# A two-layer backbone on one core: the up-projections of both feed forwards by seven products of halves

## The chip, the core and the metric

The kernel runs on one core of a Trainium2 chip. The engines of the core have queues of their own and wait for each other by semaphores: PE (TensorE) multiplies, with its weight loads shown as PEld; DVE (VectorE), ACT (ScalarE) and POOL (GpSimd) work on tiles; DMAs are issued from SP's queue. The metric is the device time of one execution in microseconds, lower is better, as the median of several runs.

## The reference

Two layers over 512 latent and 256 context tokens of width 1024. Each layer normalizes, projects, mixes the tokens in three ways, merges, and then has a gated feed forward with a convolution of width 3 along the tokens:

```python
def conv_ffn(xn, w_up, conv_w, w_down):
    u = dwconv(xn @ w_up, conv_w)
    a, gt = jnp.split(u, 2, axis=-1)
    return (a * jax.nn.silu(gt)) @ w_down
...
        h_lat = h_lat + m_lat[5] * conv_ffn(modulate(rmsnorm(h_lat, norm2_w[l]), m_lat[3], m_lat[4]),
                                            w_up[l], ffn_conv_w[l], w_down[l])
        if need_ctx:
            h_ctx = h_ctx + m_ctx[5] * conv_ffn(...)
```

w_up is 1024 x 5632 (the half a and the half of the gates), w_down 2816 x 1024. All data are float32. In the first layer the feed forward takes all 768 tokens, in the last only the 512 latent ones.

## The kernel before

A float32 product is made of three matmuls. Every operand x is split into h, its rounding to the type fp32r (a cast on ACT), and l = x - h (a subtraction on DVE, or on POOL where the code says so); the matmuls are weights h with tokens h, weights h with tokens l, weights l with tokens h, summed in one PSUM bank. `split` and `wsplit` do this; `wraw` (L213) loads the raw weights by a DMA into one of three buffers, and the halves of the weights go to two buffers each (`wh`, `wl`).

The feed forward (`ffn`) works feature-major: a block is 128 columns of w_up for all tokens. 22 blocks of gates (g) and 22 of a are done in pairs, in groups of four blocks of the hidden width (`FG`); the names are f0 or f1 for the layer, g or a, and the number of the pair's first block, with the group first: f1a42 is layer 1, a, group 4, third and fourth block. The order is g00, a00, g02, a02, g40, d0, a40, g42, a42, g80, d4, a80 and so on to a200, d16 and the tail: after the first gate pair of a group comes the down product d of the group before, added to the residual (`done_d`, L1734). The first pair, g00, is done by `gemm_first`, which takes the features one by one as the norm gives them out (`norm_fin`: t on DVE L619, xh on ACT L621, xl on DVE L622); the other 21 pairs of a layer by `gemm_fm`: for each block raw weights, split, and in `mm3` (matmuls L248 to L250) eight blocks of the contraction, three matmuls each, for 512 latent columns and in layer 0 again for 256 context columns.

```python
            for k in range(nk):
                nc.tensor.matmul(o, hv[:, k, :], xh[:, k, :], start=(k == 0), stop=False)
                nc.tensor.matmul(o, hv[:, k, :], xl[:, k, :], start=False, stop=False)
                nc.tensor.matmul(o, lv[:, k, :], xh[:, k, :], start=False, stop=(k == nk - 1))
```

A block's result is taken from PSUM by `conv`: ACT writes the middle tap (L1699), DVE adds the two others (L1700, L1702). Gates go through silu on ACT (L1708); for a, POOL multiplies with the gate (L1714), and ACT and DVE split the product into gh and gl (L1715, L1716). A scheduler orders the instructions of each engine at build time by priorities; on the chip every engine runs its list in order and waits where an operand or a buffer isn't there. In the first four pairs of layer 0's feed forward a unit of the next modulation (adp, adc) lies between.

## Time and profile before

| what | value |
|---|---|
| runs | 2727.49, 2726.53, 2725.04 us, median 2726.53 |
| span of the profiled execution | 2715.6 us |
| median of the runs above that span | 10.9 us |
| busy in the span: PE, DVE, ACT, POOL | 98%, 58%, 37%, 9% |

The profiled execution is another one than the runs; its time is given by its span, from the first to the last instruction, and the runs count 10.9 us more that lie around a span. Differences that are worked out from the trace are taken to move the runs by as much. A busy share is a mean over all stages; the feed forwards, from about 1008 to 1568 us (layer 0) and from about 2332 us to the end (layer 1), have to be looked at by themselves.

### The profile page before, as it was taken

Reading aid. Unit: us, or ns where it says so; the run is one execution under the profiler, and the core shown is the slowest. Engines: PE = TensorE matmul, PEld = TensorE weight load, DVE = VectorE, ACT = ScalarE, POOL = GpSimd, SP = SyncE. Lnnn points to the kernel's source line nnn. Section 1 sums busy time; section 2 is a strip of 40 time slices with the busy share of each in tenths; the row PEclk is TensorE's granted clock in tenths of the full one; section 3 lists DMA queues with packets and bytes.
Section 4 is the critical chain, followed back from the end, with each engine's and each line's share of the span. In section 5 each row is a group of like instructions: output and inputs, shape, how many; then the busy total and the mean of one; then the engine's idle time right before and its main releaser. Section 6 shows DMA issues by size and latency. Waiting matters only on the chain.

```text
span 2715.6 us, 46016 instructions
## 1 busy us (share of the span) xinstructions
PE 2663.0 (98%) x18041; PEld 2261.6 (83%) x18041; DVE 1573.4 (58%) x3527; ACT 998.5 (37%) x2269; POOL 235.0 (9%) x234
## 2 busy tenths in 40 slices
...
DMA packets 523466, 342.97 MB, mean 126 GB/s; under 512 B 48007, under 2 KB 488561, under 8 KB 522481
## 3 DMA queue, kind: packets, MB, share of 16 engines
...
## 4 chain that ended last, share of the span: by engine, by line
PE 88%; DMA 5%; DVE 3%; ACT 1%; issue 1%; SPq 1%; POOL 0%; DVEq 0%; ACTq 0%; POOLq 0%
PE mg04p L249 2%; PE mg04p L250 2%; PE adp L467 2%; PE mg04p L248 2%; PE y0p L248 1%; PE y0p L250 1%; PE y0p L249 1%; PE mg14p L248 1%; PE mg14p L250 1%; PE mg14p L249 1%; PE y1p L248 1%; PE y0op L248 1%; PE y0op L250 1%; PE y0op L249 1%; PE y1p L249 1%
## 5 line engine op out<-in xcount | busy, mean ns | idle before, releaser
L1714 POOL TENSOR_TENSOR f0a<-f0a,f0g 128x768 f32<-128x768 f32 x22 | 40.7, 1848 | 486.8 <-DVE f0a L1702 486.8
L467 PE MATMUL adp<-ad,s 128*32 128x128 f32 x1280 | 65.5, 283 | 2.7 <-DVE cz0t L903 2.4
L1714 POOL TENSOR_TENSOR f1a<-f1a,f1g 128x512 f32<-128x512 f32 x22 | 28.5, 1294 | 315.4 <-DVE f1a L1702 284.4
L467 PEld LDWEIGHTS adp<-ad,s 128*32 128x32 f32 x1280 | 33.9, 110 | 26.0 <-issue 9.9
L1716 DVE TENSOR_TENSOR f0gl<-f0a,f0gh 128x768 fp32r<-128x768 f32 x22 | 21.1, 959 | 58.4 <-ACT f0gh L1715 58.4
L1715 ACT CAST f0gh<-f0a 128x768 fp32r<-128x768 f32 x22 | 18.3, 832 | 76.6 <-POOL f0a L1714 76.6
L1638 POOL TENSOR_TENSOR y0a<-y0a,y0g 128x768 f32<-128x768 f32 x16 | 33.0, 2062 | 129.9 <-DVE y0g L1635 127.6
L470 ACT COPY adr<-adp 128x128 f32<-128x128 f32 x80 | 21.2, 265 | 39.7 <-PE adp L467 39.3
L901 ACT ACTIVATE mg0t<-mg04p 128x512 f32<-128x512 f32 (+1 forms) x40 | 19.4, 486 | 38.5 <-PE mg04p L250 28.2
L1708 ACT ACTIVATE f0g<-f0g 128x768 f32<-128x768 f32 x22 | 18.5, 845 | 33.2 <-DVE f0g L1702 33.2
L1638 POOL TENSOR_TENSOR y1a<-y1a,y1g 128x512 f32<-128x512 f32 x16 | 23.9, 1494 | 78.3 <-DVE y1g L1635 78.3
L491 DVE TENSOR_REDUCE ada<-adc 128x2 f32<-128x8 f32 x80 | 12.9, 161 | 27.9 <-PE adc L489 27.6
L1635 DVE SCALAR_TENSOR_TENSOR y0g<-y0g,y0p 128x512 f32<-128x512 f32 (+1 forms) x32 | 17.4, 549 | 15.7 <-PE y0p L250 14.7
L1708 ACT ACTIVATE f1g<-f1g 128x512 f32<-128x512 f32 x22 | 13.8, 631 | 32.9 <-DVE f1g L1702 32.9
L979 DVE SCALAR_TENSOR_TENSOR m0mb<-m0mb,g0a,cst 128x128 f32<-128x128 f32 x48 | 14.0, 346 | 18.4 <-DMA m0mb<-g0rd 18.4
L489 PE MATMUL adc<-cst,adr 128*128 128x128 f32 x80 | 22.2, 278 | 0.4 <-ACT adr L470 0.4
L1659 DVE SCALAR_TENSOR_TENSOR hr<-y0op,y0gh,hr 128x512 f32<-128x512 f32 (+1 forms) x16 | 9.8, 615 | 21.0 <-PE y0op L250 21.0
L1002 PE MATMUL m0n<-m0vb,m0mb 128*128 128x129 f32 x96 | 19.1, 299 | 1.1 <-issue 1.1
L1611 DVE TENSOR_TENSOR y0l<-y0ld,y0h 128x768 fp32r<-128x768 f32 x12 | 13.0, 1093 | 12.2 <-ACT y0h L1610 12.2
L1734 DVE SCALAR_TENSOR_TENSOR hr<-f0d8p,ada,hr 128x512 f32<-128x512 f32 (+1 forms) x16 | 9.9, 618 | 15.7 <-PE f0d8p L250 15.7
L1734 DVE SCALAR_TENSOR_TENSOR hr<-f0d12p,ada,hr 128x512 f32<-128x512 f32 (+1 forms) x16 | 9.9, 618 | 15.7 <-PE f0d12p L250 15.7
L1734 DVE SCALAR_TENSOR_TENSOR hr<-f0d4p,ada,hr 128x512 f32<-128x512 f32 (+1 forms) x16 | 9.9, 618 | 15.7 <-PE f0d4p L250 15.7
...
## 6 DMA issues: line engine op xcount, KB each, us to landing
...
```

The lines of the kernel that those rows point to most:

```text
L248: nc.tensor.matmul(o, hv[:, k, :], xh[:, k, :], start=(k == 0), stop=False)
L249: nc.tensor.matmul(o, hv[:, k, :], xl[:, k, :], start=False, stop=False)
L250: nc.tensor.matmul(o, lv[:, k, :], xh[:, k, :], start=False, stop=(k == nk - 1))
L467: nc.tensor.matmul(ps[32 * j:32 * j + 32, 0:128], self.s32[:, 2 * k:2 * k + 32], raw[:, k, :], start=(k < 4), stop=(k >= 4), tile_position ...
L470: nc.scalar.copy(rw, ps[:, 0:128])
L489: nc.tensor.transpose(ps[:, 128:256], rw, self.ident)
L901: nc.scalar.activation(s, o, AF.Tanh, scale=0.5)
L1638: nc.gpsimd.tensor_tensor(out=a[:, :nt], in0=a[:, :nt], in1=gt[:, :nt], op=ALU.add)
L1708: nc.scalar.activation(a[:, :nt], a[:, :nt], AF.Silu)
L1714: nc.gpsimd.tensor_tensor(out=a[:, :nt], in0=a[:, :nt], in1=keep[b][:, :nt], op=ALU.mult)
L1716: nc.vector.tensor_tensor(out=gl[:, k, :nt], in0=a[:, :nt], in1=gh[:, k, :nt].bitcast(F32), op=ALU.subtract)
L1734: nc.vector.scalar_tensor_tensor(out=hv[:, a:b], in0=ps, scalar=self.ada[l][:, 40 + j, (a >= SEQ):(a >= SEQ) + 1], in1=hv[:, a:b], op0=ALU ...
```

## The change

A pair of blocks is one product of a matrix of 2 x 2 blocks: the contraction in two halves (k blocks 0 to 3 and 4 to 7), the columns in two (the blocks r0 and r1), and the tokens in two (t0, t1; 384 each in layer 0, 256 in layer 1). `gemm7` does it in seven products of halves, after Strassen, in place of eight, with twelve matmuls each. For this POOL makes sums of the weights' halves (`half`, L314: s23 twice, r1 in place, s4, of 128x512 each), which are split like other weights: w0 = r0, w23, w1 = r1 of 1024 columns, w4 of 512. The products go to the PSUM banks x1, x6, x7, x5, and five additions on DVE (L348, L350, L354, L356, L358) and two copies on ACT (L346, L352) make the two blocks c in SBUF from them, which `conv` (now L1795, L1796, L1798) reads. The sums of the tokens are made once per layer: `norm_fin` writes the unsplit features too (L721, on POOL), `norm_sums` makes the sums T of them (eight subtractions, L620) and splits them (four times 128 x 2nt on ACT and DVE). `wh` and `wl` get a third buffer; the slots of 3072 columns become twelve of 1536 (`q6`); `first_weights` puts its weights into `wh` and `wl`. Comments are removed, and `dynamic_dma_scratch_size=1024` is set.

```diff
+class Blocks:
+
+    def __init__(self, tiles, a, b):
+        self.tiles, self.a, self.b = tiles, a, b
+
+    def __getitem__(self, i):
+        _, k, t = i
+        a = self.a + (t.start or 0)
+        b = self.b if t.stop is None else self.a + t.stop
+        return self.tiles[k // 2][:, k % 2, a:b]
...
-    def y12(self, name, dt=F32):
-        return self.P([128, 3072], name, "y12", 4, dt)
-
-    def acc(self, name, dt=F32):
-        return self.P([128, 3072], name, "acc", 2, dt)
+
+    def q6(self, name, dt=F32):
+        return self.P([128, 1536], name, "q6", 12, dt)
+
+    def pairs(self, name, n, dt=F32):
+
+        return [self.q6(f"{name}{i}", dt).rearrange("p (k t) -> p k t", k=2) for i in range(n)]
...
-            h = self.T([128, 1024], f"{nm}h", F32R, tag="wh", bufs=2)
-            l = self.T([128, 1024], f"{nm}l", F32R, tag="wl", bufs=2)
+            h = self.T([128, 1024], f"{nm}h", F32R, tag="wh", bufs=3)
+            l = self.T([128, 1024], f"{nm}l", F32R, tag="wl", bufs=3)
...
+    def gemm7(self, src, c0, x, nt, done, nm):
+        nc = self.nc
+        n = nt // 2
+        xh, xl, th, tl = x
+        r0, r1 = [self.wraw(src[:, c0 + 128 * b:c0 + 128 * b + 128], KD, 128, f"{nm}r{b}") for b in range(2)]
+        s23 = self.P([128, KD, 128], f"{nm}s23", "s23", 1)
+        s4 = self.P([128, 4, 128], f"{nm}s4", "s4", 1)
+        lo, hi = slice(0, 4), slice(4, 8)
+        def half(out, a, b, op):
+            with self.high(self.prio):
+                nc.gpsimd.tensor_tensor(out=out, in0=a, in1=b, op=op)
+        half(s23[:, hi], r0[:, lo], r1[:, lo], ALU.subtract)
+        half(r1[:, lo], r1[:, lo], r1[:, hi], ALU.add)
+        half(s23[:, lo], r1[:, lo], r0[:, lo], ALU.subtract)
+        half(s4, r0[:, hi], s23[:, lo], ALU.subtract)
+        w0 = self.wsplit(r0, KD, 128, f"{nm}w0")
+        w23 = self.wsplit(s23, KD, 128, f"{nm}w23")
+        w1 = self.wsplit(r1, KD, 128, f"{nm}w1")
+        w4 = self.wsplit(s4, 4, 128, f"{nm}w4")
+        def prod(ps, w, o, h, l, start, stop):
+            mm = lambda a, b, **kw: nc.tensor.matmul(ps, a, b, skip_group_check=True, **kw)
+            for k in range(4):
+                mm(w[0][:, o + k, :], h(k), start=(start and k == 0), stop=False)
+                mm(w[0][:, o + k, :], l(k), start=False, stop=False)
+                mm(w[1][:, o + k, :], h(k), start=False, stop=(stop and k == 3))
+        def of(t, k0, c):
+            return [lambda k, v=v: v[:, k0 + k, c] for v in t]
+        def oft(p0, c):
+            return [lambda k, v=v: v[p0 + k // 2][:, k % 2, c] for v in (th, tl)]
+        t0, t1 = slice(0, n), slice(n, nt)
+        x1, x7 = self.pl(f"{nm}x1")[:, 0:n], self.pl(f"{nm}x7")[:, 0:n]
+        x6, x5 = self.pb(f"{nm}x6")[:, 0:n], self.pb(f"{nm}x5")[:, 0:n]
+        c = [self.st(f"{nm}c{b}") for b in range(2)]
+        u = self.st(f"{nm}u")
+        p1, u2, u3 = u[:, 0:n], u[:, n:2 * n], c[1][:, 0:n]
+        add = dict(op=ALU.add)
+        prod(x1, w0, 0, *of((xh, xl), 0, t0), True, True)
+        nc.scalar.copy(p1, x1)
+        prod(x6, w23, 0, *oft(2, t1), True, True)
+        nc.vector.tensor_tensor(out=u2, in0=x6, in1=p1, **add)
+        prod(x7, w23, 4, *oft(0, t1), True, True)
+        nc.vector.tensor_tensor(out=u3, in0=x7, in1=u2, **add)
+        prod(x1, w0, 4, *of((xh, xl), 4, t0), False, True)
+        nc.scalar.copy(c[0][:, t0], x1)
+        prod(x5, w1, 0, *oft(0, t0), True, True)
+        nc.vector.tensor_tensor(out=c[1][:, t1], in0=x5, in1=u3, **add)
+        prod(x7, w1, 4, *oft(2, t0), False, True)
+        nc.vector.tensor_tensor(out=c[1][:, t0], in0=x7, in1=u2, **add)
+        prod(x5, w4, 0, *of((xh, xl), 4, t1), False, True)
+        nc.vector.tensor_tensor(out=c[0][:, t1], in0=x5, in1=u2, **add)
+        for b in range(2):
+            done(b, [(c[b][:, a:e], (a, e)) for a, e in ((0, SEQ), (SEQ, nt)) if e > a])
+            self.ada_next()
...
+        xh, xl, xs = self.x48(nm, nt)
+        self.N = dict(nm=nm, l=l, which=which, acc=self.st(f"{nm}acc"), xs=xs, x=(xh, xl), nt=nt)
+        if which:
+            self.N["raw"] = self.pairs(f"{nm}R", 4)
...
+    def norm_sums(self):
+        nc, N = self.nc, self.N
+        nt, nm, R = N["nt"], N["nm"], N["raw"]
+        t0, t1 = slice(0, nt // 2), slice(nt // 2, nt)
+        def sub(out, a, b):
+            nc.vector.tensor_tensor(out=out, in0=a, in1=b, op=ALU.subtract)
+        th, tl = [None] * 4, [None] * 4
+        def split(i):
+            th[i], tl[i] = [self.pairs(f"{nm}T{v}{i}", 1, F32R)[0] for v in "hl"]
+            self.split(th[i][:, :, :nt], tl[i][:, :, :nt], R[i][:, :, :nt])
+        for p in range(2):
+            a, b = R[p], R[p + 2]
+            sub(a[:, :, t0], a[:, :, t1], a[:, :, t0])
+            sub(a[:, :, t1], b[:, :, t1], a[:, :, t1])
+            sub(b[:, :, t1], b[:, :, t1], a[:, :, t0])
+            sub(b[:, :, t0], b[:, :, t0], b[:, :, t1])
+        for i in (2, 3, 0, 1):
+            split(i)
+        return (*N["x"], th, tl)
...
+            if "raw" in N:
+                nc.gpsimd.tensor_scalar(out=N["raw"][j // 2][:, j % 2, a:b], in0=t, scalar1=B[:, j, s:s + 1],
+                                        scalar2=None, op0=ALU.add)
...
-            gh = self.y12(f"{nm}gh{f0}", F32R).rearrange("p (k t) -> p k t", k=4)
-            gl = self.y12(f"{nm}gl{f0}", F32R).rearrange("p (k t) -> p k t", k=4)
+            gh, gl = [], []
...
                 def done_a(b, ps):
                     a = conv(f0 + p0 + b, ps, f"a{f0}{p0}{b}")
-                    k = p0 + b
+                    if b == 0:
+                        gh.extend(self.pairs(f"{nm}gh{f0}{p0}", 1, F32R))
+                        gl.extend(self.pairs(f"{nm}gl{f0}{p0}", 1, F32R))
+                    h = gh[-1][:, b, :nt]
                     nc.gpsimd.tensor_tensor(out=a[:, :nt], in0=a[:, :nt], in1=keep[b][:, :nt], op=ALU.mult)
-                    nc.scalar.copy(gh[:, k, :nt], a[:, :nt])
-                    nc.vector.tensor_tensor(out=gl[:, k, :nt], in0=a[:, :nt], in1=gh[:, k, :nt].bitcast(F32),
-                                            op=ALU.subtract)
-
-                n = min(2, fn - p0)
+                    nc.scalar.copy(h, a[:, :nt])
+                    nc.vector.tensor_tensor(out=gl[-1][:, b, :nt], in0=a[:, :nt], in1=h.bitcast(F32), op=ALU.subtract)
+
                 if f0 + p0 == 0:
                     self.gemm_first(KD, xs, done_g, f"{nm}g{f0}{p0}")
+                    x7 = self.norm_sums()
                 else:
-                    self.gemm_fm(U, D_FF + 128 * (f0 + p0), 128 * n, KD, xs, done_g, f"{nm}g{f0}{p0}")
+                    self.gemm7(U, D_FF + 128 * (f0 + p0), x7, nt, done_g, f"{nm}g{f0}{p0}")
                 if down and f0 + FG < NFF:
                     self.gemm_fm(*down)
                     down = None
-                self.gemm_fm(U, 128 * (f0 + p0), 128 * n, KD, xs, done_a,
-                             f"{nm}a{f0}{p0}")
-            segs = [((a, b), gh[:, :, a:b], gl[:, :, a:b]) for a, b in segb]
+                self.gemm7(U, 128 * (f0 + p0), x7, nt, done_a, f"{nm}a{f0}{p0}")
+            segs = [((a, b), Blocks(gh, a, b), Blocks(gl, a, b)) for a, b in segb]
```

On DVE, layer 1, from the end of pair a40 on (before; L205 is a low half of weights, L1716 gl, L1700 and L1702 the conv, whose second operand f1..p is the PSUM bank):

```order
L205 TENSOR_TENSOR f1a42s0l<-f1a42r_24754,f1a42s0h 128x1024
L1700 SCALAR_TENSOR_TENSOR f1g_24713<-f1g42p_0_24688,vec,f1g_24713 128x511
L1716 TENSOR_TENSOR f1gl_24373<-f1a_24675,f1gh_24372 128x512
L1702 SCALAR_TENSOR_TENSOR f1g_24713<-f1g42p_0_24688,vec,f1g_24713 128x511
L205 TENSOR_TENSOR f1a42s1l<-f1a42r_24792,f1a42s1h 128x1024
L1700 SCALAR_TENSOR_TENSOR f1g_24749<-f1g42p_0_24724,vec,f1g_24749 128x511
L1702 SCALAR_TENSOR_TENSOR f1g_24749<-f1g42p_0_24724,vec,f1g_24749 128x511
L205 TENSOR_TENSOR f1g80s0l<-f1g80r_24832,f1g80s0h 128x1024
L1700 SCALAR_TENSOR_TENSOR f1a_24785<-f1a42p_0_24760,vec,f1a_24785 128x511
L1702 SCALAR_TENSOR_TENSOR f1a_24785<-f1a42p_0_24760,vec,f1a_24785 128x511
```

and in the changed kernel, in pair g42 (L218 are low halves of weights, L1815 is gl, L1796 and L1798 the conv, of c; x is a PSUM bank, u and c are in SBUF):

```order
L348 TENSOR_TENSOR f1g42u<-f1g42x_25400,f1g42u 128x256
L1798 SCALAR_TENSOR_TENSOR f1a_25356<-f1a40c_25262,vec,f1a_25356 128x511
L218 TENSOR_TENSOR f1g42w4l<-f1g42s_25377,f1g42w4h 128x512
L1798 SCALAR_TENSOR_TENSOR f1a_25365<-f1a40c_25263,vec,f1a_25365 128x511
L350 TENSOR_TENSOR f1g42c_25403<-f1g42x_25399,f1g42u 128x256
L354 TENSOR_TENSOR f1g42c_25403<-f1g42x_25401,f1g42c_25403 128x256
L218 TENSOR_TENSOR f1a42w0l<-f1a42r_25506,f1a42w0h 128x1024
L1815 TENSOR_TENSOR f1gl_25361<-f1a_25356,f1gh_25360 128x512
L356 TENSOR_TENSOR f1g42c_25403<-f1g42x_25399,f1g42u 128x256
L218 TENSOR_TENSOR f1a42w23l<-f1a42s_25510,f1a42w23h 128x1024
L1815 TENSOR_TENSOR f1gl_25361<-f1a_25365,f1gh_25360 128x512
L358 TENSOR_TENSOR f1g42c_25402<-f1g42x_25401,f1g42u 128x256
```

Additions from PSUM now stand between the low halves of the next weights, and the conv reads c.

On POOL, layer 1, the products with the gates were all that it had in the pairs:

```order
L1714 TENSOR_TENSOR f1a_24637<-f1a_24637,f1g_24405 128x512
L1714 TENSOR_TENSOR f1a_24675<-f1a_24675,f1g_24441 128x512
L1714 TENSOR_TENSOR f1a_24785<-f1a_24785,f1g_24713 128x512
L1714 TENSOR_TENSOR f1a_24823<-f1a_24823,f1g_24749 128x512
L1714 TENSOR_TENSOR f1a_25095<-f1a_25095,f1g_24863 128x512
```

and now from pair g42's halves on (r are the raw weights, s is s23 or s4):

```order
L314 TENSOR_TENSOR f1g42s_25376<-f1g42r_25372,f1g42r_25374 128x512
L314 TENSOR_TENSOR f1g42r_25374<-f1g42r_25374 128x512
L314 TENSOR_TENSOR f1g42s_25376<-f1g42r_25374,f1g42r_25372 128x512
L314 TENSOR_TENSOR f1g42s_25377<-f1g42r_25372,f1g42s_25376 128x512
L314 TENSOR_TENSOR f1a42s_25510<-f1a42r_25506,f1a42r_25508 128x512
L314 TENSOR_TENSOR f1a42r_25508<-f1a42r_25508 128x512
L314 TENSOR_TENSOR f1a42s_25510<-f1a42r_25508,f1a42r_25506 128x512
L1813 TENSOR_TENSOR f1a_25356<-f1a_25356,f1g_25062 128x512
L314 TENSOR_TENSOR f1a42s_25511<-f1a42r_25506,f1a42s_25510 128x512
L1813 TENSOR_TENSOR f1a_25365<-f1a_25365,f1g_25067 128x512
L314 TENSOR_TENSOR f1g80s_25650<-f1g80r_25646,f1g80r_25648 128x512
L314 TENSOR_TENSOR f1g80r_25648<-f1g80r_25648 128x512
```

The four halves of a pair stand ahead of or between the products of the pair before.

On DVE, layer 0, between the last step of the norm (L723, before L622) and the first addition of a00, the changed kernel has among others these (R are the unsplit features, T their sums):

```order
L620 TENSOR_TENSOR n01R_10625<-n01R_10625 128x2x384
...
L620 TENSOR_TENSOR n01R_10626<-n01R_10626,n01R_10624 128x2x384
L218 TENSOR_TENSOR f0a00w23l<-f0a00s_11317,f0a00w23h 128x1024
L620 TENSOR_TENSOR n01R_10626<-n01R_10626 128x2x384
L218 TENSOR_TENSOR f0a00w1l<-f0a00r_11315,f0a00w1h 128x1024
L218 TENSOR_TENSOR n01Tl_11298<-n01R_10625,n01Th_11297 128x1536
L218 TENSOR_TENSOR f0a00w4l<-f0a00s_11318,f0a00w4h 128x512
...
L218 TENSOR_TENSOR n01Tl_11302<-n01R_10626,n01Th_11301 128x1536
L218 TENSOR_TENSOR n01Tl_11306<-n01R_10623,n01Th_11305 128x1536
L218 TENSOR_TENSOR n01Tl_11310<-n01R_10624,n01Th_11309 128x1536
L348 TENSOR_TENSOR f0a00u<-f0a00x_11341,f0a00u 128x384
```

where before, behind the conv of g00, the conv of a00 began:

```order
L1700 SCALAR_TENSOR_TENSOR f0g_11248<-f0g00p_1_11095,vec,f0g_11248 128x255
L1702 SCALAR_TENSOR_TENSOR f0g_11240<-f0g00p_1_11094,vec,f0g_11240 128x255
L1702 SCALAR_TENSOR_TENSOR f0g_11248<-f0g00p_1_11095,vec,f0g_11248 128x255
L1700 SCALAR_TENSOR_TENSOR f0a_11312<-f0a00p_0_11262,vec,f0a_11312 128x511
L1702 SCALAR_TENSOR_TENSOR f0a_11312<-f0a00p_0_11262,vec,f0a_11312 128x511
L205 TENSOR_TENSOR f0g02s0l<-f0g02r_11417,f0g02s0h 128x1024
```

So x6 of a00, whose addition is the last row of the changed kernel, comes behind w23 and the first two T.

## Rows read from the trace of the kernel before

**Rows 1.** The page: span, and busy time by engine.

```profile
span 2715.6 us, 46016 instructions
PE 2663.0 (98%) x18041; PEld 2261.6 (83%) x18041; DVE 1573.4 (58%) x3527; ACT 998.5 (37%) x2269; POOL 235.0 (9%) x234
```

**Rows 2.** Windows of the two feed forwards, each row start:end, length, then the engines' busy time.

```profile
1060.00:1560.00 500.00, 500.00 (x3006) 433.31 (x3005) 233.80 (x350) 140.22 (x209) 36.97 (x20) 1.00 0.26 75
2360.00:2660.00 300.00, 300.00 (x1295) 242.72 (x1294) 154.01 (x197) 103.32 (x146) 25.89 (x20) 1.00 0.32 94
```

**Rows 3.** Timeline of PE at the starts of two pairs, layer 1: start, duration, engine, line.

```profile
2428.85 0.39 PE L248 MATMUL f1g42p<-n11xh,f1g42s0h 128*128 128x512 f32 x1
...
2440.05 0.39 PE L248 MATMUL f1a42p<-n11xh,f1a42s0h 128*128 128x512 f32 x1
```

**Rows 4.** Timeline of PE, context columns of a pair of layer 0.

```profile
1195.54 0.28 PE L248 MATMUL f0a42p<-n01xh,f0a42s1h 128*128 128x256 f32 x1
...
1196.50 0.28 PE L250 MATMUL f0a42p<-n01xh,f0a42s1l 128*128 128x256 f32 x1
```

**Rows 5.** Timeline of DVE in the pairs of layer 1.

```profile
2429.90 1.23 DVE L205 TENSOR_TENSOR f1g42s1l<-f1g42r,f1g42s1h 128x1024 fp32r<-128x1024 f32 x1 [2.93 <-ACT f1g42s1h L204]
2431.05 0.68 DVE L1716 TENSOR_TENSOR f1gl<-f1a,f1gh 128x512 fp32r<-128x512 f32 x1
2431.65 0.74 DVE L1700 SCALAR_TENSOR_TENSOR f1a<-f1a40p,vec,f1a 128x511 f32<-128x511 f32 x1
...
2458.13 0.74 DVE L1700 SCALAR_TENSOR_TENSOR f1g<-f1g80p,vec,f1g 128x511 f32<-128x511 f32 x1
2458.79 0.68 DVE L1716 TENSOR_TENSOR f1gl<-f1a,f1gh 128x512 fp32r<-128x512 f32 x1
```

**Rows 6.** Lines of POOL, shapes apart: line, operation, count, busy us, mean ns, idle before.

```profile
L1714 POOL TENSOR_TENSOR f0a<-f0a,f0g 128x768 f32<-128x768 f32 x22 | 40.7, 1848 | 486.8 <-DVE f0a L1702 486.8
L1714 POOL TENSOR_TENSOR f1a<-f1a,f1g 128x512 f32<-128x512 f32 x22 | 28.5, 1294 | 315.4 <-DVE f1a L1702 284.4 <-issue 31.0
L546 POOL TENSOR_TENSOR n01acc<-n01acc,n01sq 128x256 f32<-128x256 f32 x9 | 6.6, 736 | 15.2 <-ACT n01sq L545 9.8 <-DVE n01acc L546 5.4
```

**Rows 7.** The page, costliest groups: the low half of the gate's product, layer 0.

```profile
L1716 DVE TENSOR_TENSOR f0gl<-f0a,f0gh 128x768 fp32r<-128x768 f32 x22 | 21.1, 959 | 58.4 <-ACT f0gh L1715 58.4
```

**Rows 8.** Timelines of POOL and DVE at two places of the merge, layer 0.

```profile
878.68 1.85 POOL L1638 TENSOR_TENSOR y0a<-y0a,y0g 128x768 f32<-128x768 f32 x1 [2.32 <-DVE y0g L1635]
879.15 2.46 DVE L205 TENSOR_TENSOR y0s21l<-y0r,y0s21h 128x1024 fp32r<-128x1024 f32 x1 [0.55 <-ACT y0s21h L204]
...
905.52 1.22 DVE L205 TENSOR_TENSOR y0s10l<-y0r,y0s10h 128x1024 fp32r<-128x1024 f32 x1
905.68 2.76 POOL L1638 TENSOR_TENSOR y0a<-y0a,y0g 128x768 f32<-128x768 f32 x1 [1.74 <-DVE y0g L1635]
907.45 1.02 DVE L1635 SCALAR_TENSOR_TENSOR y0g<-y0g,y0p 128x512 f32<-128x512 f32 x2 [0.71 <-issue]
```

**Rows 9.** Timeline of DVE, norm and first pair: layer 0, then layer 1.

```profile
1007.23 0.87 DVE L619 SCALAR_TENSOR_TENSOR n_0t<-hr,modA,n_0rb 128x256 f32<-128x256 f32 x2
...
1029.70 0.87 DVE L622 SCALAR_TENSOR_TENSOR n01xl<-n_512t,ada,n01xh 128x256 fp32r<-128x256 f32 x2
...
1034.11 0.87 DVE L1700 SCALAR_TENSOR_TENSOR f0g<-f0g00p,vec,f0g 128x255 f32<-128x255 f32 x2 [1.56 <-ACT f0g L1699]
1034.90 0.86 DVE L1702 SCALAR_TENSOR_TENSOR f0g<-f0g00p,vec,f0g 128x255 f32<-128x255 f32 x2
...
2330.53 0.87 DVE L619 SCALAR_TENSOR_TENSOR n_0t<-hr,modA,n_0rb 128x256 f32<-128x256 f32 x2
...
2345.62 1.27 DVE L622 SCALAR_TENSOR_TENSOR n11xl<-n_256t,ada,n11xh 128x256 fp32r<-128x256 f32 x3
```

**Rows 10.** Timeline of PE: first product of the second gate pair, layer 0, layer 1.

```profile
1049.25 0.50 PE L248 MATMUL f0g02p<-n01xh,f0g02s0h 128*128 128x512 f32 x1
...
2362.07 0.40 PE L248 MATMUL f1g02p<-n11xh,f1g02s0h 128*128 128x512 f32 x1
```

75 lines of the change are left out of this document (32 added, 43 removed).

## The prediction

> **What bounds the kernel now.** I read the page first, for the engine that is busiest, then the windows of the two feed forwards, then the timelines of PE, DVE and POOL inside them. PE is busy 98% of a span of 2715.6 us [rows 1], and in 500 us of layer 0's feed forward and 300 us of layer 1's it has no idle time at all, at a granted clock of 1.00, while DVE is busy for 233.8 and 154.0 us and POOL for 37.0 and 25.9 [rows 2]. So PE's matmuls set the time there. A pair of blocks in layer 1 takes 2440.05 - 2428.85 = 11.20 us for 48 matmuls of 512 columns [rows 3], 0.233 each; 256 columns take (1196.50 - 1195.54) / 8 = 0.120 [rows 4]. A pair of layer 0 has 48 of each, 16.9 us; 384 columns lie midway, 0.177.
>
> **What the change takes away.** A pair becomes 84 matmuls of 384 columns (layer 0: 84 x 0.177 = 14.8 us) or of 256 (layer 1: 84 x 0.120 = 10.0): 2.1 and 1.2 us less. Over 21 pairs in each layer this is 69 us, if nothing else ends later than PE.
>
> **What it adds to DVE and POOL.** DVE steps in their start-to-start times: a low half of 1024 columns 1.15 us, of 512 (also gl) 0.60, a conv step of 511 columns 0.66 [rows 5], of 255 columns 0.39 [rows 9], gl of 768 columns 0.96 alone [rows 7], 0.88 in a row of others. POOL takes 1.29 us for 512 columns, 1.85 for 768, 0.74 for 256 [rows 6]. Per pair DVE's low halves grow from 2 x 1.15 to 3 x 1.15 + 0.60 = 4.05 us, five additions from PSUM come in (256 columns like the conv of 255, 0.39; 384 midway to 0.66, 0.53), and POOL gets four halves, 5.16 us. ACT gains 1.5 casts of 1024 and two copies; it is busy for a third of the time [rows 2], so I cost it at nothing as long as its casts are early.
>
> **The price that decides: POOL and DVE hold each other.** At 879.15 a DVE low half of 1024 columns takes 2.46 us in place of 1.23: POOL's addition began at 878.68 and ran its normal 1.85, and DVE ends a full step of its own after it. At 905.68 it is the other way: DVE was first, took its 1.22, and POOL's 1.85 became 2.76. Two DVE steps with an operand from PSUM run inside that POOL step, at 907.45, in 1.02 us for both, undisturbed [rows 8]. So DVE steps with both operands in SBUF and POOL steps take turns. In the feed forward of before they hardly meet: the conv reads PSUM and POOL is busy 8% of the time. After the change POOL works most of the time, and the conv reads the sums c, from SBUF. No row of before shows a conv step (three operands) of that kind beside POOL; the nearest is the low half above, so I count it as held. The Trainium skill (GPSIMD Engine Reference, section 1, Specifications) says that this engine's SBUF interfaces are shared with VectorE, with contention for DVE instructions that have two SBUF inputs, of whatever operation. If the conv steps ran free beside POOL, half of them hidden as the additions are below, the second pair would be 15.3 us in layer 1 and 18.1 in layer 0, a group +2.0 and -5.2, and the sum below 2736.
>
> **The sum in the steady part.** Between two down products lie four pairs; call them first to fourth after the down product. In DVE's order the low halves of the next pair stand between a pair's own additions, and the conv of a pair comes while the next runs. No preparation runs far ahead: s23 is a single buffer, two raws of three go to a pair, and w23 of the next pair needs one of three wh. So a pair that has more turns to take than PE has matmuls lasts as long as the turns. Layer 1, held steps of DVE plus POOL's:
> - second pair: low halves 4.05, four conv steps 2.64, two gl 1.20, POOL's four halves 5.16 and two products 2.58: 15.6. The five additions (2.0) fit beside POOL at best, and not at all at worst (17.6). POOL runs about half of the time, so half: 16.6.
> - third: 4.05 + 2.64 + 5.16 = 11.9, to 13.8; 12.8.
> - fourth (no halves, the next weights are those of the down product): 1.15 + 0.60 + 1.20 + 2.64 + 1.20 + 2.58 = 9.4, to 11.4; 10.4.
> - first: 2.90 of low halves and 5.16 of POOL make 8.1, to 10.1: PE's 10.0 stands.
> Together 49.8 where four pairs took 44.8: +5.0 for a group, +25 for five groups. Layer 0 in the same way: second pair 4.05 + conv (4 x 0.66 + 4 x 0.39) 4.2 + gl 1.76 + POOL 5.16 + 3.70 = 18.9, to 21.5 with five additions of 0.53; 20.2. Third 13.4 to 16.1, fourth 12.6 to 15.3, first less: with half of the additions all stay at PE's 14.8. Together 64.6 in place of 67.7: -3.1 a group, -15.5. The last pair has none behind it to prepare: -2.1 and -1.2. The down products stay as they are; their cover hides what the first pair needs.
>
> **The start of each feed forward.** Before, a00 stood ready in the weight buffers while the norm ended, and PE filled its waits with a00's matmuls; the next pair began at 1049.25 and 2362.07 [rows 10]. Now a00 can do only x1 before the sums T. On DVE these come after the norm, whose last step ended at 1030.57 in layer 0 [rows 9]; one split and two conv steps fewer stand ahead of it (2.5), so 1028.1. Then eight subtractions (0.88), 4.2 of conv, w23 and w1 (2.3), the first T (1.5 x 1.15 = 1.7): x6 starts near 1043.3. 60 matmuls and an ada unit end at 1055: 8 us later than 1049.25 less the saving already counted. To this come POOL's 24 raw copies, by the nearest row 24 x 0.74 = 17.7 us, in the 23.4 us (from 1007.23) in which DVE does the norm. Half of the norm's steps read a PSUM operand and are free to run beside them, so nothing to 17.7 is lost, and up to 5.2 by a00's halves: +8 to +31, and I take +18. In layer 1 the norm ends at 2346.9 [rows 9]; 8 x 0.60 + 2.64 + 2.3 + 1.15 later, at 2357.8, x6 starts and a00 ends at 2365.0, against 2362.07 - 1.2: +4, with 16 copies (11.8) up to +16; I take +10.
>
> **The sum.** Layer 0: -15.5 - 2.1 + 18 = +0.4. Layer 1: +25 - 1.2 + 10 = +33.8. The span goes from 2715.6 to 2749.8; the median of the runs lies 10.9 above the span of before (2726.5), so 2761, 1.3% slower. A difference under 0.2% can't be told from none here. With every bound at its low end (additions beside POOL, no loss to copies) layer 1 gives 5 x 2.7 - 1.2 + 4 = +16 and layer 0 5 x -4.4 - 2.1 + 8 = -16: 2726, no change. With every one at its high end layer 1 gives 5 x 8.9 + 16 = +60 (first pair 10.9 by waits in DVE's order) and layer 0 about +31: 2818.
>
> **Rivals.**
> - *The turns are hidden, and the kernel is faster.* In a whole layer-1 group the turns of its four pairs make 45 us and PE's 4 x 10.0 + 22 for the down product 62; only the short reach ahead keeps them from being spread. If PE stays the bound, because the steps reach further ahead than I read from the buffers, the steady part gives all: layer 0 20 x -2.1 - 2.1 + 8 = -36, layer 1 20 x -1.2 - 1.2 + 4 = -21, so 2669. It decides for faster once the second pair lasts under about 12 us in layer 1 and 16.9 in layer 0. For it: DVE's own steps without POOL are 9.9 us in the second pair. Against it: POOL is kept busy by halves just when DVE prepares, in the order shown.
> - *The waits chain.* DVE works in order: a low half that waits for POOL holds the addition behind it, that one holds its PSUM bank (x1 and x7 have two in turn, x5 and x6 three), and PE waits before it can release the weights that the next split needs. Then the upper ends hold: about 2800. For it: an addition stands between nearly all low halves. Against it: PE's own waits leave time in which POOL and DVE catch up.
> - *No change:* the low ends, near 2726.
> - *The matmuls don't get shorter.* A matmul of 256 columns comes with a weight load each and took 0.120 [rows 4], so this is out for layer 1; 384 isn't in the trace, but lies between two that are.
>
> **Chances.** The sum as worked (2735 to 2785) 0.52; chained waits 0.20; no change 0.08; hidden turns 0.20. So slower 0.72, same 0.08, faster 0.20. The range 2690 to 2815 leaves out half of the hidden case and the end of the chained one.
>
> **What would show it.** Right: PE idle in the second and third pairs of each group, above all in layer 1, waiting for low halves w23 and w1 and their DVE steps; DVE low halves of 2.4 us and POOL halves of 2 to 3 us; additions from PSUM at their 0.39; layer 0's pairs at 14.8 except the second; x6 of a00 late by 8 us or more. Wrong: PE without idle time in 1060 to 1500 and all pairs at 14.8 and 10.0, or POOL's steps at 1.29 beside conv steps at 0.66. The clock of PE, 1.00 now, could fall where PE waits; I count nothing for it, since the windows show no wait to judge by.

## The result, and the profile after

The changed kernel takes 2769.94 us (median of four runs, 2765.56 to 2774.61), the kernel before 2725.78 us in the runs that it is compared with: 1.0167 times as long, 95% interval 1.0151 to 1.0183. It is 1.7% slower; 2761 was forecast. Its profiled execution took 2765.56 us with a span of 2763.8, so that only 1.8 us lie around a span. If the same holds for the kernel before, most of the 10.9 us between its runs and its span is not time around the span: its profiled execution was some 9 us faster than its median run. The forecast adds a difference to a median and is not touched by this, but the two traces differ by 48.2 us (2763.8 - 2715.6) where the medians differ by 44.2. The page of its profile:

```profile
span 2763.8 us, 48120 instructions
PE 2623.0 (95%) x18545; PEld 2297.7 (83%) x18545; DVE 1863.5 (67%) x3845; ACT 1109.0 (40%) x2445; POOL 567.5 (21%) x442
```

PE does 40 us less than in [rows 1], and its share falls from 98% to 95%: the matmuls did get shorter, and PE now has waits. POOL's work has grown from 235 to 567 us and DVE's from 1573 to 1863, of which only a part is new instructions: a step that is held counts as busy.

A whole group of layer 1 in the steady part, cut at the first matmuls of a80, g82, a82, g120, the down product and a120 (start:end, length, busy us of PE, PEld, DVE, ACT and POOL, granted clock, DMA share, GB/s):

```profile
2511.10:2520.50 9.40, 8.79 (x73) 8.55 (x72) 6.07 (x8) 4.20 (x6) 5.42 (x4) 1.00 0.39 113
2520.50:2534.70 14.20, 11.09 (x87) 10.72 (x86) 12.30 (x15) 6.25 (x9) 10.21 (x7) 0.95 0.25 75
2534.70:2551.50 16.80, 13.79 (x97) 13.59 (x97) 15.12 (x17) 8.36 (x12) 9.15 (x6) 0.84 0.21 62
2551.50:2561.50 10.00, 10.00 (x87) 10.00 (x86) 8.81 (x15) 5.72 (x10) 3.53 (x2) 1.00 0.10 29
2561.50:2583.50 22.00, 22.00 (x99) 18.04 (x98) 14.61 (x21) 7.43 (x12) 4.84 (x4) 1.00 0.45 132
```

72.4 us, where before a group took 66.8 (four times 11.2 and 22.0). It is the middle one of three; the one ahead of it takes 70.7 and the one behind it 73.6. The down product is as it was, 22.0, with PE busy all the time. In the second and third pairs, 14.2 and 16.8 us, PE is idle for 3.1 and 3.0 us and its granted clock is 0.95 and 0.84; DVE and POOL together have 22.5 and 24.3 us of busy time there. The same in layer 0, its four pairs and then the down product:

```profile
1257.50:1318.40 60.90, 57.09 (x326) 56.44 (x325) 50.21 (x62) 27.59 (x41) 26.04 (x16) 1.00 0.16 48
1318.40:1353.40 35.00, 35.00 (x206) 31.04 (x205) 21.88 (x35) 10.10 (x15) 6.88 (x5) 1.00 0.33 99
```

95.9 us, against 67.8 and 33.4 before (101.2): the four pairs win 6.9, and 1.6 of it comes back because the first matmuls of a pair now run among the last of the one before, so that a stretch between first matmuls is not quite a pair. PE is idle for 3.8 us of the 60.9. The group ahead of this one, a40 to g80 and d4, gains less: 100.2 us against 101.4 before.

How DVE and POOL meet, behind pair g82 of layer 1 (start, duration, engine, line):

```profile
2539.18 1.21 DVE L218 TENSOR_TENSOR f1a82w1l<-f1a82r,f1a82w1h 128x1024 fp32r<-128x1024 f32 x1
2539.44 2.10 POOL L314 TENSOR_TENSOR f1g120s<-f1g120r,f1g120r 128x512 f32<-128x512 f32 x1 [2.21 <-DMA f1g120r<-w_up]
2540.31 3.49 DVE L1796 SCALAR_TENSOR_TENSOR f1g<-f1g82c,vec,f1g 128x511 f32<-128x511 f32 x2
2541.62 1.63 POOL L314 TENSOR_TENSOR f1g120r<-f1g120r 128x512 f32<-128x512 f32 x1
2543.33 1.60 POOL L314 TENSOR_TENSOR f1g120s<-f1g120r,f1g120r 128x512 f32<-128x512 f32 x1
2543.72 0.41 DVE L348 TENSOR_TENSOR f1a82u<-f1a82x,f1a82u 128x256 f32<-128x256 f32 x1
```

POOL's half begins at 2539.44 while DVE's low half runs, and takes 2.10 us in place of 1.29: it ends about one own duration after that low half. DVE's first conv step waits for it in turn, and the second for the next half: 3.49 us for the two where they take 1.40 undisturbed. The addition from PSUM at 2543.72 falls into the third half and takes its normal 0.41. What PE waits for in layer 1 (who waits for whom, us in total, times, longest):

```profile
PE f1g82x L327 <- DVE f1g82c L350: 3.1, 1, 3.1
PE f1a82x L327 <- DVE f1a82c L350: 3.0, 1, 3.0
```

L350 is the addition that reads x7's bank before x7 is used again. It stands in DVE's list behind a conv step, w4's low half and another conv step, and each of these is held by a step of POOL:

```profile
2528.74 1.76 DVE L218 TENSOR_TENSOR f1g82w4l<-f1g82s,f1g82w4h 128x512 fp32r<-128x512 f32 x1
2530.03 1.59 POOL L314 TENSOR_TENSOR f1a82s<-f1a82r,f1a82r 128x512 f32<-128x512 f32 x1
2530.43 1.75 DVE L1798 SCALAR_TENSOR_TENSOR f1a<-f1a80c,vec,f1a 128x511 f32<-128x511 f32 x1
2532.09 0.41 DVE L350 TENSOR_TENSOR f1g82c<-f1g82x,f1g82u 128x256 f32<-128x256 f32 x1
```

The low half of 512 columns takes 1.76 us (0.68 where nothing holds it, for L1716 of the same size in [rows 5]), the conv step 1.75 for its 0.74 (the first one, at 2527.37, took 1.45), and L350 ends at 2532.50. And this is how the matmuls of 256 columns go after such a wait:

```profile
2532.56 0.39 PE L327 MATMUL f1g82x<-n11Th,f1g82w1h 128*128 128x256 f32 x1 [3.11 <-DVE f1g82c L350]
...
2533.01 0.28 PE L327 MATMUL f1g82x<-n11Th,f1g82w1h 128*128 128x256 f32 x1
2533.12 0.28 PE L327 MATMUL f1g82x<-n11Tl,f1g82w1h 128*128 128x256 f32 x1
...
2533.39 0.42 PE L327 MATMUL f1g82x<-n11Th,f1g82w1h 128*128 128x256 f32 x1
2533.61 0.42 PE L327 MATMUL f1g82x<-n11Tl,f1g82w1h 128*128 128x256 f32 x1
```

0.11 us from one to the next just after it, then 0.22: PE has gone to the lower of its two clock levels (1.2 in place of 2.4 GHz).

### The profile page after: what moved, and what is told of

The parts are those of the page before. It is cut to its first block, busy times and chain, and to the rows that moved or that the text cites. A ratio compares the mean times of both kernels' runs of the same rounds, so it can differ in the third digit from the quotient of the medians.

```text
span 2763.8 us, 48120 instructions
## 1 busy us (share of the span) xinstructions
PE 2623.0 (95%) x18545; PEld 2297.7 (83%) x18545; DVE 1863.5 (67%) x3845; ACT 1109.0 (40%) x2445; POOL 567.5 (21%) x442
## 3 DMA queue, kind: packets, MB, share of 16 engines
q1 hardware_dynamic: 522961, 336.88, 41.3%
## 4 chain that ended last, share of the span: by engine, by line
PE 74%; DVE 11%; DMA 5%; issue 4%; ACT 2%; POOL 1%; SPq 1%; DVEq 0%; POOLq 0%; ACTq 0%
PE mg04p L257 2%; PE mg04p L258 2%; PE mg04p L259 2%; PE adp L539 2%; PE y0p L258 1%; PE y0p L257 1%; PE y0p L259 1%; DMA mg14r<-w_in 1%; PE mg14p L257 1%; PE mg14p L258 1%; PE mg14p L259 1%; PE y1p L257 1%; PE y1p L258 1%; PE y1p L259 1%; DVE f1a L1798 1%
## 5 line engine op out<-in xcount | busy, mean ns | idle before, releaser
L1813 POOL TENSOR_TENSOR f0a<-f0a,f0g 128x768 f32<-128x768 f32 x22 | 46.8, 2129 | 78.5 <-DVE f0a L1798 78.5
L1813 POOL TENSOR_TENSOR f1a<-f1a,f1g 128x512 f32<-128x512 f32 x22 | 36.8, 1681 | 52.9 <-DVE f1a L1798 52.2
L1735 POOL TENSOR_TENSOR y1a<-y1a,y1g 128x512 f32<-128x512 f32 x16 | 24.2, 1514 | 67.5 <-DMA y1g<-mg 48.7
L1815 DVE TENSOR_TENSOR f0gl<-f0a,f0gh 128x768 fp32r<-128x768 f32 x22 | 26.9, 1221 | 0.0
L561 PE MATMUL adc<-cst,adr 128*128 128x128 f32 x80 | 22.5, 282 | 4.3 <-ACT adr L542 4.3
L1019 POOL MEMSET m0vb<- 128x4 f32 x6 | 0.6, 105 | 101.2 <-PE m0n L1103 46.3
L1815 DVE TENSOR_TENSOR f1gl<-f1a,f1gh 128x512 fp32r<-128x512 f32 x22 | 20.9, 949 | 0.2 <-ACT f1gh L1814 0.2
L1814 ACT CAST f1gh<-f1a 128x512 fp32r<-128x512 f32 x22 | 13.7, 622 | 18.3 <-POOL f1a L1813 18.1
```

The costliest lines, as they stand in the source:

```text
L561: nc.tensor.transpose(ps[:, 128:256], rw, self.ident)
L1735: nc.gpsimd.tensor_tensor(out=a[:, :nt], in0=a[:, :nt], in1=gt[:, :nt], op=ALU.add)
L1813: nc.gpsimd.tensor_tensor(out=a[:, :nt], in0=a[:, :nt], in1=keep[b][:, :nt], op=ALU.mult)
L1814: nc.scalar.copy(h, a[:, :nt])
L1815: nc.vector.tensor_tensor(out=gl[-1][:, b, :nt], in0=a[:, :nt], in1=h.bitcast(F32), op=ALU.subtract)
```

## The experiments

The ratios are to runs of the kernel before in the same session, whose medians lie between 2721.8 and 2723.3 us; in the session of the changed kernel's own result it was 2725.8. A difference between kernels of two sessions can thus be off by some us. Times of a stretch are read from one profiled execution each.

**Halves on DVE.** One word in `half`:

```diff
-                nc.gpsimd.tensor_tensor(out=out, in0=a, in1=b, op=op)
+                nc.vector.tensor_tensor(out=out, in0=a, in1=b, op=op)
```

> The four halves of the weights of each pair are made on DVE in place of POOL; all else as in the changed kernel (2769.9 us). Theory (DVE and POOL take turns for SBUF, so 1.29 us of POOL per half are added to DVE's own time): a half costs 0.60 on DVE, so the turns of a pair shrink by 4 x 0.69 = 2.8 us where they bind; in layer 1 a group falls from 72.4 to about 66, in layer 0 from 95.9 to about 94, in all 25 to 40 us less, near 2737. Rival (DVE's own list is the bound, POOL runs beside it): DVE gets 2.4 us more per pair, so 20 to 50 us slower than the changed kernel.

2746.6 us, 1.0088 (1.0075 to 1.0101). DVE has 2.4 us more per pair and the kernel is 23 us faster than with the halves on POOL; the rival, DVE's list as the bound with POOL beside it, is out. The gain is 2 us less than the least that the theory gave. Four pairs and the down product of layer 1:

```profile
2499.20:2544.40 45.20, 40.48 (x314) 38.89 (x312) 39.07 (x58) 21.97 (x32) 6.16 (x3) 0.96 0.26 77
2544.40:2570.10 25.70, 25.43 (x121) 20.94 (x122) 20.67 (x32) 10.24 (x17) 1.30 (x2) 1.00 0.39 113
```

The four pairs took 45.2 in place of 50.4, but the down product 25.7 in place of 22.0, together 70.9; in layer 0 the group is as long as with POOL (95.8). DVE is now in use for 39.1 of 45.2 us by itself, and it waits at a half until the raw weights have landed, up to 3.4 us at a time (f1a42), which the theory had left out. So only a small part of the gain came from the steady groups, where the theory looked for it. Some 5 us of it came at the start of layer 1 (g00 to g02 in 42.9 us, 47.8 in the changed kernel), and the larger part in layer 0 outside its steady groups: from g00 to its tail 549.9 us in place of 562.6.

**No halves, and idle halves.** Two kernels with the same PE, ACT and DVE work. The first makes no sums at all (the four calls of `half` are gone); the second lets POOL make sums of the same size into tiles that nobody reads.

```diff
-        w23 = self.wsplit(s23, KD, 128, f"{nm}w23")
+        w23 = self.wsplit(r1, KD, 128, f"{nm}w23")
-        w4 = self.wsplit(s4, 4, 128, f"{nm}w4")
+        w4 = self.wsplit(r0[:, hi], 4, 128, f"{nm}w4")
```

and in the second, where the four sums stay,

```diff
-        half(r1[:, lo], r1[:, lo], r1[:, hi], ALU.add)
+        half(s23[:, hi], r1[:, lo], r1[:, hi], ALU.add)
```

> The halves of the weights are left out: w23 and w1 are both split from the raw r1 and w4 from the second half of r0, so that the sums of the weights are not computed; PE, ACT and DVE have the same work as in the changed kernel. Theory (turns): layer 1's groups fall from 72.4 to about 63 to 65 us, layer 0's from 95.9 to about 93, the start of each feed forward by a few us: near 2715. Rival 1 (the halves come late, and all waits follow from that): the same. Rival 2 (the additions from PSUM in DVE's order hold PE, whatever POOL does): within 10 us of 2770.

> As the kernel without halves, but POOL still makes four sums of 128x512 for every pair, into tiles that nobody reads; so the sums of the weights are not used. Theory (turns): POOL's steps hold DVE's all the same, 2750 to 2770 us. Rival 1 (lateness of the halves): as without them, near 2715.

2685.96 us (0.9865, 0.9847 to 0.9883) without sums, 2769.10 (1.0171, 1.0152 to 1.0189) with idle ones: the whole loss is there although nothing waits for what the four steps make. So it is not, in the main, the lateness of the halves, and not DVE's list by itself. Without them even more is saved than I gave it, 84 us. That the two totals, 2769.10 and 2769.94, agree within 1 us is chance, as the layers show. From g00 to the tail layer 1 takes 358.1 us without sums, 403.2 with idle ones and 409.9 in the changed kernel: idle sums make 45 of the 52 us, and the other 7 may be late halves. Layer 0 takes 532.9, 568.3 and 562.6: there the idle sums cost 6 us more than the real ones. Two other ways in which idle sums could act were looked for. They read the raw weights, whose buffers could come free later; but the DMA queue waits for none of these sums in layer 1's feed forward, and for two of them, 1.1 us each, in layer 0's. And they stand ahead of the gates' products in POOL's list, for which ACT waits: 12.0 us in three groups of layer 1, against 7.3 without sums. No run keeps this second way apart from the turns. One group of layer 1, its four pairs and its down product, without sums and then with idle ones:

```profile
2462.70:2504.30 41.60, 40.07 (x337) 39.86 (x336) 34.32 (x51) 23.67 (x36) 6.36 (x4) 1.00 0.29 83
2504.30:2526.30 22.00, 22.00 (x98) 18.08 (x97) 15.41 (x23) 8.35 (x12) 0.00 (x0) 1.00 0.46 132
```

```profile
2523.00:2571.00 48.00, 43.30 (x337) 42.81 (x336) 41.89 (x50) 23.08 (x36) 32.24 (x17) 0.93 0.25 72
2571.00:2593.00 22.00, 22.00 (x98) 18.06 (x97) 16.38 (x24) 8.58 (x14) 5.14 (x3) 1.00 0.45 132
```

PE is idle for 1.5 us of 41.6 in the one and for 4.7 of 48.0 in the other, where its clock is 0.93. DVE's rows tell the same: without sums

```profile
2485.04 1.21 DVE L218 TENSOR_TENSOR f1a82w23l<-f1a82r,f1a82w23h 128x1024 fp32r<-128x1024 f32 x1
2486.51 1.21 DVE L218 TENSOR_TENSOR f1a82w1l<-f1a82r,f1a82w1h 128x1024 fp32r<-128x1024 f32 x1
2487.64 1.40 DVE L1785 SCALAR_TENSOR_TENSOR f1g<-f1g82c,vec,f1g 128x511 f32<-128x511 f32 x2
```

both low halves take 1.2 and the two conv steps 1.40, and with idle sums POOL and DVE go in turn through the same stretch:

```profile
2546.59 1.97 DVE L218 TENSOR_TENSOR f1a82w23l<-f1a82r,f1a82w23h 128x1024 fp32r<-128x1024 f32 x1
2547.44 2.28 POOL L314 TENSOR_TENSOR f1a82s<-f1a82r 128x512 f32<-128x512 f32 x1
2548.81 1.98 DVE L218 TENSOR_TENSOR f1a82w1l<-f1a82r,f1a82w1h 128x1024 fp32r<-128x1024 f32 x1
2549.68 2.28 POOL L314 TENSOR_TENSOR f1a82s<-f1a82r,f1a82s 128x512 f32<-128x512 f32 x1
```

Each of the last three begins while the other engine's step ahead of it still runs and ends about one own duration (1.1 to 1.2 us) after that: 1.98 for DVE's 1.23, 2.28 for POOL's 1.29. The first does the same behind a product of POOL that ends at 2547.47.

**Half of the idle sums.** Two in place of four:

```diff
-        half(s23[:, hi], r1[:, lo], r1[:, hi], ALU.add)
-        half(s23[:, lo], r1[:, lo], r0[:, lo], ALU.subtract)
-        half(s4, r0[:, hi], s23[:, lo], ALU.subtract)
+        half(s4, r0[:, hi], s23[:, hi], ALU.subtract)
```

> As the run with four idle sums on POOL per pair (2769.1), with two of them; the sums of the weights are not used. Theory (turns): the cost goes with POOL's steps, and half of them give between 2686 (none) and 2769 (four), 2715 to 2740. Rival (it is the meeting as such, or a POOL that is nearly always busy, that costs): under 2695 or over 2755.

2706.72 us (0.9942, 0.9917 to 0.9966), 8 us under the range. The cost does go with POOL's steps, but not in proportion: the first two cost 21 us, the next two 62. A group of layer 1 is 65.9 us (63.6 without sums, 70.0 with four), and of the last 62 us 30 lie in layer 0, whose groups go from 92.9 without sums to 93.6 with two and 99.8 with four. That the first steps find time in which DVE would wait anyhow fits this, but no run shows it by itself.

**The pools alone.** Eight products everywhere, without copies and sums T:

```diff
-                    x7 = self.norm_sums()
...
-                    self.gemm7(U, D_FF + 128 * (f0 + p0), x7, nt, done_g, f"{nm}g{f0}{p0}")
+                    self.gemm_fm(U, D_FF + 128 * (f0 + p0), 256, KD, xs, done_g, f"{nm}g{f0}{p0}")
```

and the same for a.

> All 21 pairs of both layers by gemm_fm with eight products again, without the copies of the features and the sums T; the new pools, the third buffer of weights and the place of the first weights stay. In the trace of the changed kernel layer 0's feed forward began 7.1 us earlier than before (1001.3 against 1008.4). If the new slots of the merge give that by themselves: 2715 to 2722 us. Rival (it came from the order that the scheduler found with gemm7 behind it): within 2 us of before, 2726, or a little slower since a00's weights wait for a buffer.

2722.51 us against 2721.76, 0.9997 (0.9985 to 1.0008): the new slots, the third buffer and the moved first weights together cost and give nothing that can be told from the noise. That g00 of layer 0 began at 1001.3 in the changed kernel's profile was not the pools' doing: in the profiles of this study it begins anywhere from 1001.3 to 1009.6, with 1008.4 here.

**Layer 0 alone.** `gemm7`, copies and T only where l is 0:

```diff
-                    x7 = self.norm_sums()
+                    x7 = self.norm_sums() if l == 0 else None
```

> Layer 1's pairs by gemm_fm with eight products again, without its copies of the features and its sums T; layer 0 as in the changed kernel. Theory (the loss is layer 1's, 48 us from the start of its feed forward to its tail, while layer 0 is 3 us slower than before at its start and gains as much in its groups): within 4 us of the kernel before, 2720 to 2728. Rival (the two layers share the loss, since the later one only inherits what the first leaves behind): 2735 to 2755.

2721.94 against 2721.88, 0.9998 (0.9985 to 1.0010). The loss is layer 1's; layer 0 gives back at its start what its groups win.

**A later start.** a00 by eight products, the unsplit features on ACT:

```diff
+                if f0 + p0 == 0:
+                    self.gemm_fm(U, 0, 256, KD, xs, done_a, f"{nm}a00")
+                else:
+                    self.gemm7(U, 128 * (f0 + p0), x7, nt, done_a, f"{nm}a{f0}{p0}")
...
-                nc.gpsimd.tensor_scalar(out=N["raw"][j // 2][:, j % 2, a:b], in0=t, scalar1=B[:, j, s:s + 1],
-                                        scalar2=None, op0=ALU.add)
+                nc.scalar.activation(N["raw"][j // 2][:, j % 2, a:b], t, AF.Identity, bias=B[:, j, s:s + 1])
```

> The first pair a00 of both layers by gemm_fm (eight products), so that the sums T are wanted one pair later, and the unsplit features written by ACT in place of POOL; the rest as in the changed kernel (2769.9). Theory (the start costs layer 0 17 us and layer 1 17 us, by waits for T and by the lower clock that comes with them): a00 costs 2.1 and 1.2 us more on PE, the start's waits go, 22 to 30 us less, near 2743. Rival (DVE has to make the sums anyhow and the next pair waits for them instead): at most 10 us less.

2746.54 us, 1.0082 (1.0059 to 1.0105): 23 us less than the changed kernel, as the theory gave; its four runs spread from 2735.2 to 2752.4, and the profiled one is the fastest. From g00 to g02 layer 0 takes 41.3 us (58.1 in the changed kernel, 40.9 before), layer 1 36.2 (47.8, 30.4). A part of the rival is there too: from g02 to a40, the stretch behind this, layer 0 takes 103.8 us where the changed kernel took 97.9, so 6 of its 17 us come back. What each of the two edits gave, the later sums or the copies on ACT, was not tried apart.

**Both, and then without POOL.** Layer 0 alone with the later start; and the same with the halves and the products with the gates on DVE:

```diff
-                    nc.gpsimd.tensor_tensor(out=a[:, :nt], in0=a[:, :nt], in1=keep[b][:, :nt], op=ALU.mult)
+                    nc.vector.tensor_tensor(out=a[:, :nt], in0=a[:, :nt], in1=keep[b][:, :nt], op=ALU.mult)
```

> Both edits together: seven products in layer 0 alone, from g02 on, a00 by gemm_fm, the unsplit features by ACT. Theory: the start of layer 0 is as before within 4 us, its groups give 1 to 5 us each as in the changed kernel, its last pair 3: 10 to 15 us less than the kernel before, 2707 to 2713. Rival (layer 0's groups gain only because the pair before them was late): no faster than before.

> As the run with seven products in layer 0 from g02 on, and the halves of the weights and the products with the gates on DVE in place of POOL, in both layers. Theory (turns): a half costs 0.60 in place of 1.29 and a product of 768 columns 0.88 in place of 1.85, so the turns of a second pair fall from 18.9 to 14.2 us, 16.9 with its additions, and the others lie under PE's 14.8: 2 to 4 us less per group of layer 0, 2695 to 2705. Rival (DVE's list gets too long, as with the halves on DVE in both layers, where the down products grew from 22 to 25.7 us in layer 1): no better than with POOL, or worse.

2714.04 us, 0.9966 (0.9953 to 0.9979), and 2693.91 us, 0.9897 (0.9879 to 0.9915). The first is 1 us above its range: the groups win what they won before, but the first one, in which the units of the next modulation lie, takes 105.4 us (96.3 before). The second is 1 us under its range, 1.0% under the kernel before, and the fastest of the kernels here that leave nothing out. One group of layer 0 there:

```profile
1244.90:1301.90 57.00, 55.38 (x315) 54.18 (x313) 47.46 (x74) 25.44 (x39) 0.00 (x0) 1.00 0.18 52
1301.90:1339.20 37.30, 37.30 (x216) 33.24 (x217) 27.92 (x45) 11.84 (x18) 0.00 (x0) 1.00 0.32 92
```

57.0 us for four pairs and 37.3 for the down product, 94.3 in place of 101.2; DVE is busy for 47.5 us of the 57.0 with 74 steps and POOL not at all, PE waits at most 0.6 us at a time. With POOL in use the same group took 96.1 (the run before this one), so it won 1.7 us of the 2 to 4 that were forecast; more came ahead of the steady groups, 5.3 us from g02 to a40 and 3.3 in the group behind that, and 5.1 from a160 to the tail.

**All repairs in both layers:**

> Seven products in both layers with all repairs: a00 by gemm_fm, the unsplit features by ACT, the halves and the products with the gates on DVE, POOL idle in the feed forwards. Theory: in layer 1 DVE's own list per pair is 4.05 + 2.64 + 0.60 + 1.98 + 2.4 + 0.60 = 12.3 us in the mean against PE's 10.0 and 11.2 with eight products, so layer 1 loses 0 to 1 us a pair against eight products there: 2694 to 2715, no better than seven products in layer 0 alone (2694). Rival (without POOL's turns layer 1 is bound by PE, 10.0 a pair): 2670 to 2680.

2717.11 us, 0.9979 (0.9965 to 0.9993), 2 us above the theory's range; the rival, PE as the bound once POOL is gone, is out. In layer 1

```profile
2360.00:2660.00 300.00, 276.98 (x1845) 252.73 (x1846) 255.27 (x397) 137.76 (x206) 0.00 (x0) 0.98 0.31 89
```

PE is idle for 23 of 300 us with POOL at 0.00. In the four pairs a80 to g120 (45.0 us, 44.8 before) DVE is busy for 39.6, no longer than the 40 us that PE's matmuls need; but it also stands idle at the halves, 0.9 to 2.0 us at a time, until the raw weights have landed, and the steps behind them in its list come later by that. PE's longest waits, 1.9 us, are for ACT's copy of x1 (L352), which itself waits for a conv step of DVE. So it is DVE's list together with these stops that holds PE; how much the stops alone cost was not tried. Layer 1 loses with seven products even so, 23 us against the kernel that has them in layer 0 alone.

## Why the prediction held, and where its steps were off

**Turns.** The step on which the sign hung is shown: with PE, ACT and DVE work alike, four POOL steps per pair whose results nobody waits for make 2685.96 into 2769.10. The Trainium skill (GPSIMD Engine Reference, section 1, Specifications) names the sharing of SBUF interfaces for DVE instructions with two SBUF inputs; the trace agrees, and for conv steps too, for which the trace of before had no row: 3.49 us for two that take 1.40.

**The steady part of layer 1.** Forecast were 49.8 us for four pairs, measured 50.4 (9.4, 14.2, 16.8, 10.0). The parts were shared out otherwise than I had them, 10.0, 16.6, 12.8 and 10.4: x1 of the next pair runs before x5 of this one ends, and the gates' products and gl of the second pair fall partly into the third. That the sum came out so near is luck in part: the second pair had been put 2.4 us too high and the third 4.0 too low, the additions were taken as half hidden without a row for it, and the clock, which I had at 1.00, is at 0.95 and 0.84 in these two pairs (see the clock, below). The two groups beside this one took 48.7 and 51.7 us for their four pairs.

**The last group** was mis-sized: I took five like groups. In the last one g200 has the pair a200 behind it and not the down product, so halves for the next pair are made beside it too, and it takes 14.6 us; from a160 to the tail layer 1 lost 9.3 us where I had 5.0 - 1.2.

**Layer 0's groups.** Forecast -3.1 each. The two steady ones, a80 and a120 on, came out at -5.3 (95.9 against 101.2), but the one ahead of them at -1.2, the stretch from g02 to a40 at +1.6 and that from a160 to the tail, last pair included, at -3.6. So the groups as a whole gave about what was forecast, but none of them the -3.1. 384 columns take what was interpolated, 0.175 us (two matmuls from 1259.61 to 1259.96) against 0.177. In a steady group, with the 1.6 us of the down product's stretch, four pairs took 62.5 for a forecast of 64.6; which of the turns found more cover than I gave them, no run tells.

**The start** was forecast at +18 and +10 (beside the saving of a00); it is 58.14 - 40.89 + 2.1 = +19.4 in layer 0 and 47.78 - 30.41 + 1.2 = +18.6 in layer 1. The size in layer 0 was right for partly wrong reasons, and layer 1's was mis-sized by 8.6. POOL's copies of the features took 1.1 to 1.2 us each in the mean, not 0.74:

```profile
1002.90 4.81 POOL L721 TENSOR_SCALAR n01R<-n_0t,ada 128x256 f32<-128x256 f32 x4
...
1025.97 0.48 DVE L723 SCALAR_TENSOR_TENSOR n01xl<-n_512t,ada,n01xh 128x256 fp32r<-128x256 f32 x1
...
1031.43 4.87 DVE L620 TENSOR_TENSOR n01R<-n01R,n01R 128x768 f32<-128x768 f32 x3
1031.86 1.67 POOL L314 TENSOR_TENSOR f0a00s<-f0a00r,f0a00r 128x512 f32<-128x512 f32 x1
...
1044.60 8.25 DVE L218 TENSOR_TENSOR n01Tl<-n01R,n01Th 128x1536 fp32r<-128x1536 f32 x3
1045.82 2.67 POOL L314 TENSOR_TENSOR f0g02s<-f0g02r,f0g02r 128x512 f32<-128x512 f32 x1
```

Four in 4.81 us; two later ones that meet no DVE step, at 1011.39 and 1012.29, take 0.92. Yet the norm's last DVE step (1025.97) ends 25.2 us after g00's first matmul (1001.27), against 22.2 before [rows 9], where that matmul stood at 1008.36: the norm lost 3 us, and the 2.5 us of other steps that no longer stand in it, to 27.4 us of copies. Half of its steps read a PSUM operand. What cost more were the sums T behind it, three subtractions in 4.87 us beside a00's halves and three low halves in 8.25 beside g02's, and perhaps the clock, for which I had counted nothing:

```profile
1020.00:1030.00 10.00, 7.72 (x52) 6.88 (x51) 9.63 (x21) 4.95 (x10) 10.00 (x9) 1.00 0.00 1
1030.00:1040.00 10.00, 5.75 (x53) 4.03 (x51) 9.97 (x12) 7.55 (x10) 5.40 (x5) 0.91 0.44 125
1040.00:1050.00 10.00, 5.91 (x29) 4.48 (x29) 10.00 (x7) 4.49 (x4) 8.12 (x4) 0.50 0.46 134
1050.00:1060.00 10.00, 9.84 (x55) 9.30 (x56) 6.11 (x8) 2.21 (x4) 1.23 (x1) 0.73 0.15 43
2361.00:2371.00 10.00, 5.50 (x21) 4.33 (x21) 10.00 (x11) 5.68 (x8) 5.58 (x4) 0.58 0.25 73
```

The granted clock is 0.50 from 1040 to 1050 us, all of it at the lower level, after 20 us in which PE was busy for 7.7 and 5.8 of 10 each; in layer 1 it is 0.58 in the same place. At the upper level the 5.9 us of the first ten and some 5.3 of the 9.8 in the second (a mean of 0.73 is 5.4 us of ten at the lower one) would take half, so by this estimate the clock costs layer 0 at most 5.6 us here. POOL's halves are the smaller part of the start: without any of them (the run of 2685.96) it still takes 53.9 us in layer 0 and 42.8 in layer 1, 13 and 12 of the 17 us that each start lost. The later start brings 23 us back in both layers together.

**What was over.** Layer 0's feed forward came out at 562.6 us from g00 to the tail, against 559.2: +3.4 for a forecast of +0.4. Layer 1's came out at 409.9 against 361.6: +48.3 for +33.8, of which 8.6 lie in the start, 5.5 in the last group and pair. By the traces the feed forwards are thus 17.5 us over the forecast. The medians are only 9 over it (2770 against 2761): g00 of layer 0 began 7 us earlier in the changed kernel's profile, and that profile is compared here with a fast one of before. The sizes were off, and one term, the clock, had been put at nothing. The rival of hidden turns would have needed a second pair under 12 us in layer 1; it took 14.2 and the third 16.8. The chained waits are there (L350 behind three held steps), but PE's idle time stays at about 3 us per pair.

**The clock.** The groups of layer 1 ahead of the one shown above and behind it:

```profile
2440.40:2511.10 70.70, 64.34 (x433) 59.57 (x432) 56.85 (x72) 31.70 (x49) 32.77 (x20) 0.98 0.30 90
2583.50:2657.10 73.60, 67.15 (x433) 62.19 (x432) 57.87 (x72) 32.24 (x49) 32.87 (x21) 0.93 0.29 86
```

With the 72.4 us of the middle one, whose clock is 0.95 over the whole group, three groups of the same work get longer as their clock gets lower. The kernel with idle sums has the waits without the lower clock, in the group ahead of the one shown of it:

```profile
2453.10:2523.00 69.90, 62.77 (x434) 57.99 (x433) 58.79 (x72) 31.96 (x49) 38.80 (x22) 1.00 0.31 91
```

The group behind the one shown of it also takes 69.9 us at 1.00, and the one shown, at 0.95 over the whole group, takes 70.0. So in that kernel the waits alone cost 3.1 us a group against the 66.8 before, where the forecast had 5.0 for the turns, and the lower clock costs nothing that shows. In the changed kernel the three groups lose 3.9, 5.6 and 6.8. What they lose above 3.1 goes along with the clock, but the late halves, which the other kernel does not have, could cause it too.

What stays open: which of the two makes one group of the changed kernel 3 us longer than another. No run had late halves in layer 1 at a clock of 1.00 throughout.
